# The down projection of a SwiGLU feed-forward layer: eight quarter products, or seven

## The chip, the cores and the metric

One Trainium2 chip; the kernel runs on one of its cores, and all times are device times in microseconds (us). The kernel before has a median of 852.21 us over three runs (851.84 to 852.43). The input is one sequence of 512 tokens with 1024 features, in float32; the weights are float32 and lie in the chip's memory.

## The reference

One decoder layer: three token mixers with gates, a projection with a residual, and a SwiGLU feed-forward layer (FFN) with a residual. The change is in the last line but one, in the product with `ffn_w_down`, a matrix of 2816 x 1024.

```python
def rmsnorm(x, w):
    xf = x.astype(jnp.float32)
    y = xf * lax.rsqrt(jnp.mean(xf * xf, axis=-1, keepdims=True) + EPS)
    return (y * w.astype(jnp.float32)).astype(x.dtype)
...
        x = x + rmsnorm(mixed @ w_out[l], norm_mix_post[l])
        h = rmsnorm(x, norm_ffn_pre[l])
        f = (jax.nn.silu(h @ ffn_w_gate[l]) * (h @ ffn_w_up[l])) @ ffn_w_down[l]
        x = x + rmsnorm(f, norm_ffn_post[l])
```

## The kernel before

All large products are made from float32 numbers that are split into two parts, H (rounded to TensorE's fast float32 form) and L (the rest). A product of two such numbers is three matmuls: H by H, H by L and L by H. A weight chunk of 512 KB goes through `split_chunk`: SyncE issues a DMA into a `raw` buffer, of which there are three (`NRAW`), ScalarE casts it to `wH`, and VectorE subtracts that from `raw` to get `wL`; of `wH` and `wL` there are four buffers each (`NWH`). Since `raw` is read last by the VectorE subtraction, that instruction frees it for the next load.

```python
raw = wpool.tile([P, kt, nf], F32, tag="raw", name=f"raw_{name}", bufs=NRAW)
nc.sync.dma_start(raw, src.rearrange("(k p) f -> p k f", p=P))
S.copy(H, raw)
(eng or V).tensor_tensor(L, raw, H.bitcast(F32), op=ALU.subtract)
```

The FFN begins with 11 steps `u`, each of two blocks of 128 hidden features. A step loads two chunks of the gate weights and two of the up weights (`raw_ffn_w_gate`, `raw_ffn_w_up`, rows of 1 KB in memory), multiplies them with `h2` into the PSUM tiles `ff` (L190), and ends with a SiLU on ScalarE, a product on VectorE (L865) and the split of the result into `gT` (L866, L867).

Then comes the down projection. A chunk is one block of 128 hidden features with all 1024 columns (`raw_fd`, rows of 4 KB). For each of 22 chunks TensorE runs four tiles of 128 tokens x two halves of 512 columns x three parts, 24 matmuls of 128x128 by 128x512 (L201), into eight PSUM banks `dn`; the last three chunks are kept back, so that the four token tiles end one after the other and `post_norm` of a tile (square on ScalarE, power on GpSimd, two products and two sums on VectorE, L219 to L239) runs beside the matmuls of the next. The residual rows come from memory (`x1d`, two loads of 1 MB at L875) and the results go to `out` in halves of 256 KB.

A scheduler places each engine's instructions. It takes the program's order as priorities, and loads and splits of weights stand 400 places ahead of their use (`LEAD`). Each engine then works off its own list in order; SyncE's list holds the DMA issues, and an issue that waits holds up all behind it.

Of the kernel before, what the change touches and what calls it, by code (L numbers as in the profile page):

```python
# [72 lines left out]
def hybrid_block(ctx: ExitStack, tc: tile.TileContext, a: dict, out: bass.AP):
# [595 lines left out]
    def moba(u, qst, kst, vst):  # L669
# [207 lines left out]
    dn = [ps2((NF + t) % 4, f"dn{t}") for t in range(NT)]  # L877
    last = []
    for k in range(NF):
        (h, l, _, _), = load(a["ffn_w_down"][k * P:(k + 1) * P, :], f"fd{k}")  # L880
        W = [(h, l, k, 1)]
        if k >= NF - 3:
            last += W
            continue
# [37 lines left out]
```

## Time and profile before

| what | number |
|---|---|
| median of three runs | 852.21 us (851.84 to 852.43) |
| span of the profiled execution | 850.9 us, 1.3 us under that median |
| instructions | 10857 |
| TensorE busy | 835.4 us, 98% |
| VectorE busy | 411.7 us, 48% |
| ScalarE busy | 302.9 us, 36% |
| GpSimd busy | 64.5 us, 8% |
| bytes moved by DMA | 86.71 MB |

The span is from the first to the last instruction of one profiled execution. Busy times are sums over an engine's instructions without overlaps. The granted clock is the speed that TensorE was given, 1.00 being its full one.

### The profile page before, as it was taken

The page shows a single profiled execution, that of the slowest core. Times are in us where ns is not written, and L with a number is a line of the kernel's source. Part 1 is how long each engine was busy: PE and PEld are TensorE (multiplying, and loading weights), DVE is VectorE, ACT ScalarE, POOL GpSimd, SP SyncE. Part 2 cuts the span into 40 slices and gives each one's busy share as a digit, 9 for nine tenths or more (in the row PEclk, how much of TensorE's full clock was granted, in tenths as well). Part 3 has the DMA queues.
Part 4 walks back from the last instruction along what each step waited for, and adds up shares of the span by engine and source line. Part 5 has one row for each costly group of instructions (what it writes and reads, how often), then busy time and mean ns, then how long its engine had stood idle before and what let it go on. Part 6 is the DMA issues. An engine that isn't in the chain of part 4 may idle for free.

```text
span 850.9 us, 10857 instructions
## 1 busy us (share of the span) xinstructions
PE 835.4 (98%) x4436; PEld 720.8 (85%) x4436; DVE 411.7 (48%) x635; ACT 302.9 (36%) x471; POOL 64.5 (8%) x61
## 2 busy tenths in 40 slices
PE   5999999999999999999999999999999999999997
PEld 5889998889888877888899998888888888888885
DVE  4639957766477564334446553333333333322225
ACT  5354324554455332223344343332222332211112
POOL 2200012110010003112111000000000000000001
PEclk9999999999999999999999999999999999999999
DMA  8421322221322632333351533333333333333302
GB/s 297 124 75 51 84 65 75 75 75 52 100 76 79 217 99 75 99 99 99 99 164 70 172 115 100 99 99 99 100 99 96 94 98 121 113 99 99 99 25 100
DMA packets 70100, 86.71 MB, mean 102 GB/s; under 512 B 3217, under 2 KB 63394, under 8 KB 70050
## 3 DMA queue, kind: packets, MB, share of 16 engines
q1 hardware_dynamic: 70050, 86.01, 33.0%
q8 instruction: 35, 0.57, 0.3%
q14 instruction: 15, 0.12, 0.0%
HBM read 81.81 MB, written 4.19 MB: 101 GB/s over the span
## 4 chain that ended last, share of the span: by engine, by line
PE 96%; DVE 1%; DMA 1%; ACT 0%; POOL 0%; issue 0%; SPq 0%; DVEq 0%; POOLq 0%; ACTq 0%
PE ff L190 28%; PE dn L201 14%; PE ow L201 5%; PE pga L190 5%; PE pgb L190 5%; PE pgc L190 5%; PE gv L201 3%; PE mv L201 3%; PE pya L190 3%; PE mq L190 3%; PE pu L190 3%; PE mk L190 3%; PE pyb L190 3%; PE gqk L190 3%; PE pyc L190 3%; PE gr L201 1%
## 5 line engine op out<-in xcount | busy, mean ns | idle before, releaser
L190 PE MATMUL ff<-h2H,wL_ffn_w_up 128*128 128x512 f32 (+1 forms) x192 | 71.4, 372 | 0.0
L190 PE MATMUL ff<-h2L,wH_ffn_w_up 128*128 128x512 f32 (+1 forms) x192 | 71.3, 372 | 0.0
L190 PE MATMUL ff<-h2L,wH_ffn_w_gate 128*128 128x512 f32 (+1 forms) x192 | 71.2, 371 | 0.0
L190 PE MATMUL ff<-h2H,wL_ffn_w_gate 128*128 128x512 f32 (+1 forms) x192 | 71.2, 371 | 0.0
L190 PE MATMUL ff<-h2H,wH_ffn_w_up 128*128 128x512 f32 (+1 forms) x192 | 71.2, 372 | 0.0
L190 PE MATMUL ff<-h2H,wH_ffn_w_gate 128*128 128x512 f32 (+1 forms) x192 | 71.0, 371 | 0.0
L138 DVE TENSOR_TENSOR wL_fd<-raw_fd,wH_fd 128x1024 fp32r<-128x1024 f32 x22 | 27.0, 1225 | 87.7 <-ACT wH_fd L137 87.7
L138 DVE TENSOR_TENSOR wL_ffn_w_gate<-raw_ffn_w_gate,wH_ffn_w_gate 128x1024 fp32r<-128x1024 f32 x22 | 26.9, 1225 | 75.5 <-ACT wH_ffn_w_gate L137 75.5
L201 PE MATMUL dn<-wH_fd,gTH 128*128 128x512 f32 x160 | 62.2, 389 | 0.0
L201 PE MATMUL dn<-wL_fd,gTH 128*128 128x512 f32 x160 | 62.2, 389 | 0.0
L201 PE MATMUL dn<-wH_fd,gTL 128*128 128x512 f32 x160 | 62.1, 389 | 0.0
L137 ACT CAST wH_fd<-raw_fd 128x1024 fp32r<-128x1024 f32 x22 | 23.2, 1054 | 89.4 <-PE dn L201 74.1
L138 DVE TENSOR_TENSOR wL_ffn_w_up<-raw_ffn_w_up,wH_ffn_w_up 128x1024 fp32r<-128x1024 f32 x22 | 27.0, 1225 | 41.7 <-ACT wH_ffn_w_up L137 41.7
L137 ACT CAST wH_ffn_w_gate<-raw_ffn_w_gate 128x1024 fp32r<-128x1024 f32 x22 | 23.1, 1052 | 56.1 <-issue 34.3
L190 PEld LDWEIGHTS ff<-h2L,wH_ffn_w_up 128*128 128x128 f32 x192 | 36.2, 188 | 6.3
L190 PEld LDWEIGHTS ff<-h2L,wH_ffn_w_gate 128*128 128x128 f32 x192 | 36.2, 188 | 6.3
L190 PEld LDWEIGHTS ff<-h2H,wH_ffn_w_up 128*128 128x128 f32 x192 | 36.1, 188 | 6.3
L190 PEld LDWEIGHTS ff<-h2H,wL_ffn_w_gate 128*128 128x128 f32 x192 | 36.2, 188 | 6.2
L190 PEld LDWEIGHTS ff<-h2H,wL_ffn_w_up 128*128 128x128 f32 x192 | 36.2, 188 | 6.1
L190 PEld LDWEIGHTS ff<-h2H,wH_ffn_w_gate 128*128 128x128 f32 x192 | 36.0, 188 | 6.3
L137 ACT CAST wH_ffn_w_up<-raw_ffn_w_up 128x1024 fp32r<-128x1024 f32 x22 | 23.2, 1053 | 48.8 <-PE ff L190 47.7
L201 PEld LDWEIGHTS dn<-wH_fd,gTH 128*128 128x128 f32 x160 | 30.0, 188 | 6.3
(328 smaller groups left out, 2093.3 us busy)
## 6 DMA issues: line engine op xcount, KB each, us to landing
raw_ffn_w_gate<-in_ffn_w_gate_dram SPq DMA_DIRECT2D x22, 512.0 KB, 3.7
raw_ffn_w_up<-in_ffn_w_up_dram SPq DMA_DIRECT2D x22, 512.0 KB, 3.7
raw_fd<-in_ffn_w_down_dram SPq DMA_DIRECT2D x22, 512.0 KB, 3.4
raw_gatea<-in_w_in_dram SPq DMA_DIRECT2D x8, 512.0 KB, 3.6
raw_gateb<-in_w_in_dram SPq DMA_DIRECT2D x8, 512.0 KB, 3.6
raw_gatec<-in_w_in_dram SPq DMA_DIRECT2D x8, 512.0 KB, 3.5
raw_wo<-in_w_out_dram SPq DMA_DIRECT2D x8, 512.0 KB, 3.5
raw_gv<-in_w_in_dram SPq DMA_DIRECT2D x4, 512.0 KB, 3.5
```

Of the source, the lines that this page charges most:

```text
L137: S.copy(H, raw)
L138: (eng or V).tensor_tensor(L, raw, H.bitcast(F32), op=ALU.subtract)
L190: PE.matmul(ps, lhsT=w[:, k, f * P:(f + 1) * P], rhs=m(k0 + k, lo, hi), start=n == 0 and i == 0, stop=n == len(W) - 1 and i == len(seq) - 1)
L201: PE.matmul(ps, lhsT=m(k0 + k, lo, hi), rhs=w[:, k, c0:c1], start=first and n == 0 and i == 0, stop=last and n == len(W) - 1 and i == len( ...
```

## The change

The down projection is cut into quarters: tokens into two halves of 256, hidden features into two halves of 1408 (11 blocks), columns into two halves of 512. Instead of the eight products of an activation quarter with a weight quarter, seven are made, of sums and differences of quarters: p1, p5, p6, p7, p2, p3, p4 in program order. Each has 11 blocks x two token tiles x three parts, 66 matmuls of the form before, so 462 in place of 528. A chunk of a product is now two blocks by 512 columns (the last one block), again 512 KB, in rows of 2 KB, and is used by 12 matmuls.

Sums of weight quarters are made on VectorE in float32, before the split: t1 of two loads (L946, for p5), t2 = t1 plus a load (L950, for p6), t3 of two loads (L955, for p7), t4 = t2 plus a load (L959, for p4). t1, t2 and t4 stay in a tile `tau`; t3 is made in the raw buffer itself. p1, p2 and p3 use a loaded quarter as it is. The activations stay float32 (`ga`, L893); their sums and differences (L966, L977, L982, L1003) and their splits into H and L (`Quarter.put`: ScalarE L872, VectorE L873) are made in groups of 4, 4 and 3 blocks. p1, p6 and p7 accumulate in the same two PSUM banks, from which ScalarE copies what stands there after each (L972, L987, L991). The residual loads stand at L1020, and `finish` calls `post_norm` for two tiles ahead of p4 and two behind it.

```diff
 NRAW, NWH = 3, 4
 LEAD = 400
 G1W = RANK + 256
+TH = T // 2
+KH = NF // 2
+KGROUPS = ((0, 4), (4, 8), (8, KH))
...
-    def post_norm(pss, wrow, res, dst, name, then):
+    def post_norm(pss, wrow, res, dst, name, then, order=(0, 1)):
+        pss = [pss[c] for c in order]
         rs = rstd_of(pss, [t2(f"sq_{name}_{c}") for c in range(2)], name)
-        sls = [slice(0, T), slice(T, D)]
+        sls = [(slice(0, T), slice(T, D))[c] for c in order]
...
-    gT = Pair(NF, "gT")
+    ga = {(z, i): slot([P, hi - lo, T], f"ga{z}{i}") for z in range(2) for i, (lo, hi) in enumerate(KGROUPS)}
+    def quarter(tz, z, i):
+        return ga[z, i][:, :, tz * TH:(tz + 1) * TH]
+    class Quarter:
...
+        def put(self, i, src):
+            S.copy(self.t[i][:, 0], src)
+            V.tensor_tensor(self.t[i][:, 1], src, self.t[i][:, 0].bitcast(F32), op=ALU.subtract)
...
             S.activation(sg, ff[f][0], AF.Silu)
-            V.tensor_tensor(sg, sg, ff[f][1], op=ALU.mult)
-            S.copy(gT.h(k), sg)
-            V.tensor_tensor(gT.l(k), sg, gT.h(k).bitcast(F32), op=ALU.subtract)
+            V.tensor_tensor(ga[z, r // 4][:, r % 4, :], sg, ff[f][1], op=ALU.mult)
+            if z == 0 and r + 1 in [hi for _, hi in KGROUPS]:
+                a11.put(r // 4, quarter(0, 0, r // 4))
...
+    chunks = [(lo, min(lo + 2, KH)) for lo in range(0, KH, 2)]
...
+    def product(name, X, ps, src, start, group=1):
+        done = []
+        for n, (lo, hi) in enumerate(chunks):
+            with tc.high_priority(offset=LEAD):
+                w = src(n)
+                h = wpool.tile([P, 2, T], F32R, tag="wH", name=f"wH_{name}{n}", bufs=NWH)[:, 0:hi - lo]
+                l = wpool.tile([P, 2, T], F32R, tag="wL", name=f"wL_{name}{n}", bufs=NWH)[:, 0:hi - lo]
+                S.copy(h, w)
+                V.tensor_tensor(l, w, h.bitcast(F32), op=ALU.subtract)
+            done.append((lo, hi, h, l))
+            if n + 1 < len(chunks) and n >= len(chunks) - group:
+                continue
+            for j in range(2):
+                for lo_, hi_, h_, l_ in done:
+                    for k in range(lo_, hi_):
+                        for i, (z, w_) in enumerate(((0, h_), (0, l_), (1, h_))):
+                            PE.matmul(ps[j], lhsT=X.part(z, k, j), rhs=w_[:, k - lo_, :],
+                                      start=start and k == 0 and i == 0, stop=k == KH - 1 and i == 2,
+                                      skip_group_check=True)
+            done = []
+    def raw_of(z, c, name):
+        def src(n):
+            lo, hi = chunks[n]
+            r = wpool.tile([P, 2, T], F32, tag="raw", name=f"raw_{name}{n}", bufs=NRAW)[:, 0:hi - lo]
+            nc.sync.dma_start(r, wq(z, c, lo, hi))
+            return r
+        return src
+    tau = [slot([P, hi - lo, T], f"tau{n}") for n, (lo, hi) in enumerate(chunks)]
+    def t1_of(n):
+        V.tensor_tensor(tau[n], raw_of(0, 0, "t1a")(n), raw_of(0, 1, "t1b")(n), op=ALU.add)
+        return tau[n]
+    def t2_of(n):
+        V.tensor_tensor(tau[n], tau[n], raw_of(1, 1, "t2")(n), op=ALU.add)
+        return tau[n]
+    def t3_of(n):
+        r = raw_of(1, 1, "t3a")(n)
+        V.tensor_tensor(r, r, raw_of(0, 1, "t3b")(n), op=ALU.add)
+        return r
+    def t4_of(n):
+        V.tensor_tensor(tau[n], tau[n], raw_of(1, 0, "t4")(n), op=ALU.add)
+        return tau[n]
+    pa, pc, pd = ps2(0, "pa"), ps2(1, "pc"), ps2(2, "pd")
...
+    for i in NG:
+        V.tensor_tensor(s1[i], quarter(1, 1, i), quarter(1, 0, i), op=ALU.subtract)
+        qs1.put(i, s1[i])
+    product("p1", a11, pa, raw_of(0, 0, "p1"), True)
+    a11.free()
+    cp = [slot([P, 2, T], "c_p")]
+    for j in range(2):
+        S.copy(cp[0][:, j], pa[j])
+    product("p5", qs1, pc, t1_of, True)
...
+    for i in NG:
+        V.scalar_tensor_tensor(s1[i], s1[i], -1.0, quarter(0, 0, i), ALU.mult, ALU.subtract)
+        qs2.put(i, s1[i])
+    product("p6", qs2, pa, t2_of, False)
+    qs3 = Quarter("qs3_")
+    for i in NG:
+        V.tensor_tensor(quarter(0, 0, i), quarter(0, 0, i), quarter(1, 0, i), op=ALU.subtract)
+        qs3.put(i, quarter(0, 0, i))
...
+    for j in range(2):
+        S.copy(cp[1][:, j], pa[j])
+    qs2.free()
+    product("p7", qs3, pa, t3_of, False)
+    for j in range(2):
+        S.copy(cp[2][:, j], pa[j])
+        V.scalar_tensor_tensor(cp[2][:, j], pc[j], -1.0, cp[2][:, j], ALU.mult, ALU.subtract)
...
+    product("p2", a12, pd, raw_of(1, 0, "p2"), True)
...
+    for j in range(2):
+        V.tensor_tensor(cp[0][:, j], pd[j], cp[0][:, j], op=ALU.add)
...
+        V.scalar_tensor_tensor(s1[i], s1[i], -1.0, quarter(0, 1, i), ALU.mult, ALU.subtract)
+        qs4.put(i, s1[i])
...
+    product("p3", qs4, pc, raw_of(1, 1, "p3"), False)
...
-    for t in range(NT):
+    def finish(t, parts, order):
         z = slot([P, D], f"z_{t}")
...
+    for t in range(2):
+        finish(t, [cp[0][:, t], cp[1][:, t]], (0, 1))
+    product("p4", a22, pa, t4_of, False, 2)
+    for t in range(2):
+        finish(2 + t, [pa[t], cp[2][:, t]], (1, 0))
```

The scheduler decides where the new instructions stand. SyncE's list before, at the first loads of the down projection (`raw_fd`, one load a chunk; behind each row, what it waits for: an earlier transfer's landing, or an engine):

```order
L136 DMA raw_fd0_0_5871<-in_ffn_w_down_dram 128x1024 [waits DMAHW0_49,DVE_49]
L136 DMA raw_fd1_0_5901<-in_ffn_w_down_dram 128x1024 [waits DMAHW1_49,DVE_49]
L136 DMA raw_fd2_0_5931<-in_ffn_w_down_dram 128x1024 [waits DMAHW2_49,DVE_49]
L136 DMA raw_fd3_0_5961<-in_ffn_w_down_dram 128x1024 [waits DMAHW3_49,DVE_49]
L136 DMA raw_fd4_0_5991<-in_ffn_w_down_dram 128x1024 [waits DMAHW4_49,DVE_49]
```

And SyncE's list now, from the last load of p1 into those of p5 (`t1a` and `t1b` with a chunk's number, the two quarters of which t1 is the sum):

```order
L939 DMA raw_p15_5928<-in_ffn_w_down_dram 128x512 [waits DMAHW3_49,DVE_49]
L939 DMA raw_t1a0_5942<-in_ffn_w_down_dram 128x2x512 [waits DMAHW4_49,DVE_49]
L939 DMA raw_t1b0_5944<-in_ffn_w_down_dram 128x2x512 [waits DMAHW5_49,DVE_49]
L939 DMA raw_t1a1_5963<-in_ffn_w_down_dram 128x2x512 [waits DMAHW6_49,DVE_49]
L939 DMA raw_t1b1_5965<-in_ffn_w_down_dram 128x2x512 [waits DMAHW7_49,DVE_49]
L939 DMA raw_t1a2_5984<-in_ffn_w_down_dram 128x2x512 [waits DMAHW0_49]
L939 DMA raw_t1b2_5986<-in_ffn_w_down_dram 128x2x512 [waits DMAHW1_49,DVE_49]
```

A chunk of p5 takes two of the three raw buffers; the issue of `t1a2` needs the same VectorE instruction as that of `t1b1` before it, and has no wait for VectorE of its own.

VectorE's list now, from the end of p1's splits (`wL_p15`) to the first split of p5 (`wL_p50`) and a little beyond; `qs2_`, `s1_` and `ga` are activation quarters, `tau` the sums of weights:

```order
L922 TENSOR_TENSOR wL_p15_5931<-raw_p15_5928,wH_p15_5930 128x512 [waits DMAHW6_49,Activation_49]
L982 TENSOR_TENSOR ga01_4275<-ga01_4275 128x4x256 [waits DVE_49]
L873 TENSOR_TENSOR qs2_0_6062<-two_s1_0_5824,qs2_0_6062 128x1024 [waits PE_49,Activation_49]
L982 TENSOR_TENSOR ga02_4276<-ga02_4276 128x3x256 [waits DVE_49]
L946 TENSOR_TENSOR two_tau0_5815<-raw_t1a0_5942,raw_t1b0_5944 128x1024 [waits DMAHW7_49,DMAHW0_49]
L873 TENSOR_TENSOR qs2_1_6063<-two_s1_0_5824,qs2_1_6063 128x1024 [waits Activation_49]
L1003 SCALAR_TENSOR_TENSOR two_s1_0_5824<-two_s1_0_5824,ga10_4277 128x1024 [waits DVE_49]
L922 TENSOR_TENSOR wL_p50_5948<-two_tau0_5815,wH_p50_5947 128x1024 [waits Activation_49]
L1003 SCALAR_TENSOR_TENSOR two_s1_0_5824<-two_s1_0_5824,ga11_4278 128x1024 [waits DVE_49]
L946 TENSOR_TENSOR two_tau0_5815<-raw_t1a1_5963,raw_t1b1_5965 128x1024 [waits DMAHW2_49,DMAHW1_49]
L873 TENSOR_TENSOR qs2_2_6064<-two_s1_2_5825,qs2_2_6064 128x768 [waits PE_49,Activation_49]
L1003 SCALAR_TENSOR_TENSOR two_s1_2_5825<-two_s1_2_5825,ga12_4279 128x768 [waits DVE_49]
```

Before, the same engine had one subtraction a chunk in this stage; now sums and splits of activation quarters that p6 and p3 need stand between p1's last split and p5's first.

SyncE's list now, from the last loads of p7 to those of p2 (`x1_0`, 1 MB, is the residual of the first two token tiles):

```order
L939 DMA raw_t3a5_6302<-in_ffn_w_down_dram 128x512 [waits DMAHW3_49,DVE_49]
L939 DMA raw_t3b5_6304<-in_ffn_w_down_dram 128x512 [waits DMAHW2_49,DVE_49]
L1020 DMA x1_0_6560<-x1d_3725 128x2x1024 [waits DMAHW5_49,PE_49]
L939 DMA raw_p20_6330<-in_ffn_w_down_dram 128x2x512 [waits DVE_49]
L939 DMA raw_p21_6348<-in_ffn_w_down_dram 128x2x512 [waits DMAHW7_49,DMAHW4_49,DVE_49]
```

Before, the residual's first half was loaded during the FFN's first part and its second among the first chunks of the down projection; now the first stands ahead of p2's first chunk, and the second a few loads behind.

## Rows read from the trace of the kernel before

**Rows 1.** The page: each engine's busy us, share of the span and instructions.

```profile
PE 835.4 (98%) x4436; PEld 720.8 (85%) x4436; DVE 411.7 (48%) x635; ACT 302.9 (36%) x471; POOL 64.5 (8%) x61
```

**Rows 2.** The chain of waits at the end: start us, us, what.

```profile
725.09 119.69 PE dn L201 x528
...
844.87 0.60 ACT sq_pf L219
...
845.87 0.59 POOLq L918
...
846.48 0.75 DVE two_z L239
847.23 0.66 DVEq L918
```

**Rows 3.** Table by stretch: down projection, part of the FFN, the end.

```profile
core 0: us, PE busy (x) PEld busy (x) DVE busy (x) ACT busy (x) POOL busy (x), PEclk, DMA share, GB/s
724.93:844.77 119.84, 119.84 (x529) 98.91 (x527) 33.83 (x41) 25.38 (x34) 1.65 (x3) 1.00 0.25 83
495.00:724.00 229.00, 229.00 (x1061) 191.74 (x1060) 81.47 (x87) 71.27 (x89) 0.00 (x0) 1.00 0.35 102
840.00:851.00 11.00, 4.77 (x22) 3.61 (x20) 5.41 (x12) 2.06 (x6) 1.10 (x2) 0.90 0.37 142
```

**Rows 4.** Waits of SyncE's queue: line, for what; total us, times, longest us.

```profile
SPq L136 <- DVE wL_fd L138: 92.5, 19, 5.7
```

**Rows 5.** Landings of raw_fd, then of raw_ffn_w_gate; SyncE's timeline, start and us.

```profile
L136 SPq DMA_DIRECT2D raw_fd<-in_ffn_w_down_dram x22: 327/328/340, 694.6 to 809.1; - x22
...
DMA to landing us min/median/max: 3.1/3.4/5.4
...
L136 SPq DMA_DIRECT2D raw_ffn_w_gate<-in_ffn_w_gate_dram x22: 367/368/384, 439.4 to 678.3; - x22
...
DMA to landing us min/median/max: 3.5/3.7/5.4
...
719.68 0.38 SPq L875 DMA_DIRECT2D x<-x1d  x1
721.80 0.33 SPq L136 DMA_DIRECT2D raw_fd<-in_ffn_w_down_dram  x1
raw_fd<-in_ffn_w_down_dram SPq DMA_DIRECT2D x1, 512.0 KB, 5.4
```

**Rows 6.** Splits and casts in pairs (timeline), then groups by shape with mean ns.

```profile
430.76 1.22 DVE L138 TENSOR_TENSOR wo2L<-raw_wo,wo2H 128x1024 fp32r<-128x1024 f32 x1 [4.63 <-ACT wo2H L137]
431.91 1.22 DVE L138 TENSOR_TENSOR wL_wo<-raw_wo,wH_wo 128x1024 fp32r<-128x1024 f32 x1
...
429.68 1.05 ACT L137 CAST wo2H<-raw_wo 128x1024 fp32r<-128x1024 f32 x1 [2.32 <-DMA raw_wo<-in_w_out_dram]
430.64 1.05 ACT L137 CAST wH_wo<-raw_wo 128x1024 fp32r<-128x1024 f32 x1
...
L138 DVE TENSOR_TENSOR wL_fd<-raw_fd,wH_fd 128x1024 fp32r<-128x1024 f32 x22 | 27.0, 1225 | 87.7 <-ACT wH_fd L137 87.7
L865 DVE TENSOR_TENSOR sg<-sg,ff 128x512 f32<-128x512 f32 x22 | 15.1, 687 | 13.0 <-PE ff L190 12.9
L867 DVE TENSOR_TENSOR gTL<-sg,gTH 128x512 fp32r<-128x512 f32 x20 | 13.7, 688 | 6.2 <-ACT gTH L866 6.2
```

**Rows 7.** DMA issues with us to landing; the DMA's rate from 8 to 20 us.

```profile
out_dram<-two_z SPq DMA_DIRECT2D x6, 256.0 KB, 2.0
...
DMA packets 3895, 4.55 MB, mean 379 GB/s; under 512 B 700, under 2 KB 3407, under 8 KB 3895
```

**Rows 8.** VectorE's timeline at the end: start us, us.

```profile
845.67 0.69 DVE L237 TENSOR_TENSOR two_z<-dn,two_wp 128x512 f32<-128x512 f32 x1
846.48 1.41 DVE L239 SCALAR_TENSOR_TENSOR two_z<-two_z,rs_pf,x 128x512 f32<-128x512 f32 x2
```

More of the change, by code (lines that the diff above doesn't have):

```diff
@@ L851, in hybrid_block, with __init__, part, free @@
     free("xr_0", "xr_2", "wn", "wo2H", "wo2L", "wo3H", "wo3L")
-    gT = Pair(NF, "gT")
+    ga = {(z, i): slot([P, hi - lo, T], f"ga{z}{i}") for z in range(2) for i, (lo, hi) in enumerate(KGROUPS)}
+    def quarter(tz, z, i):
+        return ga[z, i][:, :, tz * TH:(tz + 1) * TH]
+    class Quarter:
+        def __init__(self, name):
+            self.t = [slot([P, 2, hi - lo, TH], f"{name}{i}", F32R) for i, (lo, hi) in enumerate(KGROUPS)]
+            self.names = [f"{name}{i}" for i in range(len(KGROUPS))]
+        def put(self, i, src):
+            S.copy(self.t[i][:, 0], src)
+            V.tensor_tensor(self.t[i][:, 1], src, self.t[i][:, 0].bitcast(F32), op=ALU.subtract)
+        def part(self, z, k, j):
+            return self.t[k // 4][:, z, k % 4, j * P:(j + 1) * P]
+        def free(self):
+            free(*self.names)
+    a11 = Quarter("a11")
     for u in range(NF // 2):
@@ L869, in hybrid_block, with wq @@
     h2.free()
+    wd = a["ffn_w_down"]
+    chunks = [(lo, min(lo + 2, KH)) for lo in range(0, KH, 2)]
+    NG = range(len(KGROUPS))
+    def wq(z, c, lo, hi):
+        r = (z * KH + lo) * P
+        return wd[r:r + (hi - lo) * P, c * T:(c + 1) * T].rearrange("(k p) f -> p k f", p=P)
+    def product(name, X, ps, src, start, group=1):
[18 more added lines that the diff above has]
+            done = []
@@ new lines, in t3_of @@
+    def t3_of(n):
[6 more added lines that the diff above has]
+    pa, pc, pd = ps2(0, "pa"), ps2(1, "pc"), ps2(2, "pd")
+    s1 = [slot([P, hi - lo, TH], f"s1_{i}") for i, (lo, hi) in enumerate(KGROUPS)]
+    qs1 = Quarter("qs1_")
+    for i in NG:
+        V.tensor_tensor(s1[i], quarter(1, 1, i), quarter(1, 0, i), op=ALU.subtract)
+        qs1.put(i, s1[i])
@@ new lines, in hybrid_block @@
+    product("p1", a11, pa, raw_of(0, 0, "p1"), True)
[4 more added lines that the diff above has]
+    product("p5", qs1, pc, t1_of, True)
+    qs1.free()
+    qs2 = Quarter("qs2_")
+    for i in NG:
[6 more added lines that the diff above has]
+        qs3.put(i, quarter(0, 0, i))
@@ new lines, in hybrid_block @@
+    free(*[f"ga0{i}" for i in NG])
+    cp += [slot([P, 2, T], "c_u2"), slot([P, 2, T], "c_u3")]
+    for j in range(2):
[5 more added lines that the diff above has]
+        V.scalar_tensor_tensor(cp[2][:, j], pc[j], -1.0, cp[2][:, j], ALU.mult, ALU.subtract)
+    a12 = Quarter("a12")
+    for i in NG:
+        a12.put(i, quarter(0, 1, i))
+    product("p2", a12, pd, raw_of(1, 0, "p2"), True)
@@ new lines, in hybrid_block @@
+    a12.free()
+    qs3.free()
+    for j in range(2):
+        V.tensor_tensor(cp[0][:, j], pd[j], cp[0][:, j], op=ALU.add)
+    qs4 = Quarter("qs4_")
+    for i in NG:
+        V.scalar_tensor_tensor(s1[i], s1[i], -1.0, quarter(0, 1, i), ALU.mult, ALU.subtract)
+        qs4.put(i, s1[i])
+    free(*[f"s1_{i}" for i in NG])
+    product("p3", qs4, pc, raw_of(1, 1, "p3"), False)
+    for j in range(2):
+        V.scalar_tensor_tensor(cp[1][:, j], pc[j], -1.0, cp[1][:, j], ALU.mult, ALU.subtract)
@@ L870, in hybrid_block @@
+    qs4.free()
+    a22 = Quarter("a22")
+    for i in NG:
+        a22.put(i, quarter(1, 1, i))
+    free(*[f"ga1{i}" for i in NG])
     wp = slot([P, D], "wp")
@@ L876, in hybrid_block @@
         x1 += [xt[:, 0], xt[:, 1]]
[L877 to L884, printed above, removed]
-        for t in range(NT):
-            for c in range(2):
-                mm_tm(dn[t][c], gT, t, W, c * T, (c + 1) * T, k == 0, False)
-    for t in range(NT):
-        for c in range(2):
-            mm_tm(dn[t][c], gT, t, last, c * T, (c + 1) * T, False, True)
-    for t in range(NT):
-        z = slot([P, D], f"z_{t}")
-        post_norm(dn[t], wp, x1[t], z, f"pf{t}",
-                  lambda sl: nc.sync.dma_start(out[t * P:(t + 1) * P, sl], z[:, sl]))
+    def finish(t, parts, order):
+        z = slot([P, D], f"z_{t}")
+        post_norm(parts, wp, x1[t], z, f"pf{t}",
+                  lambda sl: nc.sync.dma_start(out[t * P:(t + 1) * P, sl], z[:, sl]), order)
+    for t in range(2):
[3 more added lines that the diff above has]
+        finish(2 + t, [pa[t], cp[2][:, t]], (1, 0))
 _INS = ["x", "norm_mix_pre", "w_in", "gla_w_g2", "gla_b_g", "gla_norm", "pool_w", "pool_scale",
```

1 line of the change is left out of this document (added).

## The prediction, made from the kernel before

> **What bounds the kernel now.** I read the page first: TensorE is busy for 98% of the span and VectorE for 48% [rows 1]. Next the chain of waits: the down projection is one unbroken piece of 528 matmuls in 119.69 us, so one matmul of 512 columns costs 119.69 / 528 = 0.2267 us of the path, although each is recorded with 389 ns, because they overlap; after its last matmul the chain runs through a square, a power and two sums of one tile [rows 2]. The table by stretch says the same of the engines there: TensorE 119.84 of 119.84 us, VectorE 33.83, ScalarE 25.38, all at a granted clock of 1.00, and DMA at a share of 0.25 [rows 3]. So this stage is bound by TensorE alone, and work beside it is free while it keeps up.
>
> Then what feeds TensorE. SyncE, which issues the loads, waited 19 times for the VectorE split that frees a raw buffer, the longest 5.7 us: it is paced by the 24 matmuls (5.44 us) of a chunk [rows 4]. A load lands 3.1, 3.4 or 5.4 us (shortest, median, longest) after its issue with rows of 4 KB, and 3.5, 3.7, 5.4 with rows of 1 KB [rows 5]. One split of 128x1024 on VectorE takes 1.225 us; two in a row start 1.15 us apart (430.76, 431.91), and the ScalarE casts 0.96 us apart [rows 6].
>
> **What it removes.** 528 matmuls become 7 x 66 = 462 of the same 512 columns. 66 x 0.2267 = 15.0 us. Two ScalarE casts and VectorE splits per FFN tile pair also change, but those engines have room there (VectorE 81.47 of 229 us, [rows 3]), which I cost at nothing: the cover is TensorE at 229.00 of 229.00.
>
> **What it adds, product by product.** The program order of TensorE is p1, p5, p6, p7, p2, p3, p4, each 66 x 0.2267 = 14.96 us if fed. A chunk is now 12 matmuls, 2.72 us, in place of 24, and p5 and p7 need two loads and one VectorE add for each chunk. Only three raw buffers exist. Two hold the pair being added and the third the first half of the next pair; the second half (t1b, t3b) can be issued only when the add has freed a buffer. So add, load, add, load is one serial loop: 1.225 (the add, by the split's row of like size) + 0.03 + 3.5 (landing, with rows of 2 KB between 3.4 and 3.7) = 4.75 us a chunk against TensorE's 2.72. The last chunk is half as big: 0.69 (the 128x512 row, [rows 6]) + 0.03 + 2.7 (estimate: between 2.0 for the stores of 256 KB, [rows 7], and 3.5) = 3.4 us.
>
> - *p1*: its first chunks are split before the FFN ends; no loss.
> - *p5*: the last product of the FFN (L893) waits for the FFN's last matmul, so it stands at p1's start; one difference is ahead of it and 15 instructions behind it up to the first split of p5 (the third fence of the change shows the end of that row of work). Of the 17, eleven have 1024 elements at 1.15, four 768 at 0.88 (estimate between 0.61 and 1.15), two 512 at 0.61 (0.688 less the 0.07 by which two overlap): 17.4 us, and TensorE needs 14.96 for p1. The split is 2.3 us late. The second add has two quarter operations ahead of it: 1.1 us more. Then four loops of 4.75, one of 3.4, and 0.9 for the last four matmuls: 2.3 + 1.1 + 19.0 + 3.4 + 0.9 = 26.7 us in place of 14.96, **+11.7**.
> - *p6*: one load per chunk, but VectorE has to add (5 x 1.15 + 0.61 = 6.4), split (6.4), split five pieces of later quarters that stand between (3 x 1.15 + 2 x 0.88 = 5.2) and finish p5's last split (0.6): 18.6 us against 14.96, **+3.7**.
> - *p7*: the same loop as p5. Its first add stands about 5 us ahead of p6's end, since VectorE is a chunk and a half (4.1 us) ahead of TensorE plus one split. From that add: four loops and the short one (22.4), then add, cast and split of the half chunk (2.0) and 0.9 of matmuls, less 5.0: 20.3 us, **+5.3**.
> - *p2*: SyncE's queue now has a 1 MB load of x1 between the last t3 loads and p2's first one (the fourth fence of the change). That chunk is issued after p7's fifth split, lands after 3.5 + 0.7 (a share of the 2.8 us that 1 MB takes at 379 GB/s, [rows 7]), is cast 1.05 and split 1.225: 6.5 us, while TensorE has 3.7 us of p7 left and 0.4 of matmuls that need the cast only: **+2.4**.
> - *p3, p4*: one load a chunk at 1.15 + 1.15 us of VectorE work and few quarters; 2.72 us of TensorE covers them: no loss. Each of p2, p3 and p4 then needs 2.88 MB in 15 us, half of 379 GB/s.
> - *Tail*: before, one tile is finished after the last matmul (844.77 to 850.9, 6.1 us, [rows 3]). Now two tiles end within two matmuls of each other, and the second one's product and two sums (0.69 + 1.41, [rows 8]) stand behind the first's on VectorE: between 0 and 2.3 us, taken as **+1.9**, nearer the upper end because both wait for the last two matmuls.
>
> Sum: -15.0 + 11.7 + 3.7 + 5.3 + 2.4 + 1.9 = +10.0 us. On the profiled span of 850.9 that is 860.9. The median of the runs shown is 852.21, 1.3 us over that span; with the same 1.3 the forecast is **862.2 us**, 1.2% slower.
>
> **Bounds.** The loop runs eight times in full and twice at half size, counted as nine. With the shortest landing, 3.1, it costs 9 x 0.4 = 3.6 us less; with the longest, 5.4, 17 us more. The raw_fd that took 5.4 us was issued at 721.80, two us after a 1 MB load (719.68, [rows 5]), so loads that meet others are late, and here they come in pairs; half of that, +8, is my upper end. VectorE's 1024-element operations on the quarters read rows of 256 in place of 1024; no row has this form, and I keep the price of the split, since where the operand lies did not matter in two other forms (128x512 from PSUM 687 ns, from SBUF 688, [rows 6]). Its other uncertain pieces (p6, the 1.1) move 3 us either way.
>
> **Rivals.**
> 1. *Not slower: the loads run ahead and the loop never closes.* If SyncE gets far enough ahead during p1, and the loop costs less than TensorE's chunk, only p6, p2, the first split and the tail remain: -15.0 + 3.7 + 2.4 + 2.3 + 1.9 = -4.7, 847.5 us; without the first three too, 839. The point from which it decides: -15.0 + 10.3 leaves 4.7 us for ten loops, so a loop under 2.72 + 0.5 = 3.2 us, a landing under 2.0. The trace has no 512 KB load under 3.1 [rows 5]. For it: the queue was idle for three quarters of this stage before [rows 3]. Chance 0.07.
> 2. *The pairs land late.* Every second load comes right behind another, as that 5.4 us one did; the loop is then 5.7 to 6.6 us. At +1.0 for nine loops and p2: 872 us. For it: 5.4 also is the longest of the FFN's loads. Against: the second of a pair has a whole loop of time. Chance 0.14.
> 3. *TensorE's clock falls.* In p5 and p7 it would be idle for 2 of each 4.75 us. The granted clock is 1.00 over the whole stage before, its level of 2.4 GHz, and 0.90 over the last 11 us, in which TensorE is busy for 4.77 and then has stopped for good [rows 3]; no row shows it with work in short bursts. The Trainium skill (TensorE: Matmul & The Clock Gate, "HAM oscillation — how this bites in real kernels") describes a kernel whose loop over chunks waited for a load each time, and whose clock fell at every chunk; no run here shows that so far. At 1.2 GHz twelve matmuls would cost 5.4 us, over the loop's 4.75, so p5 and p7 would take 30 us each (+3.3, +9.6): 875 us. Against: the idle pieces are about 2 us, with 2.7 us of work between them. Chance 0.05.
>
> The forecast itself has 0.74. That VectorE alone would bind is no case of its own: over the seven products it has some 110 us of work (44 of splits, 25 of adds, 19 of quarter splits, 13 of quarter sums, 10 of the rest, at the prices above) against TensorE's 105, and a part of it runs before p1. Where it binds most, in p6, it is in the sum.
>
> **How the numbers follow.** The forecast reaches from 856 (short landings, p6 cheaper) to 869; adding rival 2 up to 872 and a little of the low side gives 855 to 872, which leaves out most of rivals 1 and 3 and the upper half of 2: some 0.18. A measurement here tells 0.2%, 1.7 us, from no change. Faster: 0.06; same: 0.02; slower: 0.92.
>
> **What would show it.** In the changed kernel's profile the window of p5 and p7 should have TensorE idle between chunks with VectorE's split as releaser, SyncE waiting for the adds (L946, L955), issues of t1b 4.5 to 5 us apart, VectorE busy for nearly all of p6, p3 and p4 with TensorE full, and 462 down matmuls. A p5 of under 18 us breaks the loop; landings over 4.5 us speak for rival 2, a granted clock under 1.00 between p5 and p7 for rival 3. It is wrong altogether if TensorE stays full through p5.

## The result, and the profile after

The changed kernel takes 873.62 us (median of four runs, 872.37 to 875.19) against 852.04 us for the kernel before on the same chip (median of four now): a ratio of 1.0253, 95% interval 1.0239 to 1.0266. It is slower, as forecast, but by twice as much: the profiled span went from 850.9 to 870.6 us, +19.7, where the sum had +10.0, and 873.62 lies above the range of 855 to 872.

The table by stretch of the changed kernel, one row for each product (p1, p5, p6, p7, p2, p3, p4, in TensorE's order) and one for the tail; it answers to [rows 3]. A row is 66 matmuls in TensorE's order; at the end of p5 two of p6's stand ahead of p5's last four, so that border is sharp to half a microsecond only:

```profile
core 0: us, PE busy (x) PEld busy (x) DVE busy (x) ACT busy (x) POOL busy (x), PEclk, DMA share, GB/s
724.28:739.24 14.96, 14.96 (x68) 12.33 (x66) 14.96 (x16) 7.73 (x9) 0.00 (x0) 1.00 0.35 107
739.24:766.01 26.77, 17.98 (x67) 11.53 (x67) 19.66 (x19) 10.35 (x12) 0.00 (x0) 1.00 0.60 209
766.01:785.97 19.96, 15.77 (x67) 12.04 (x65) 19.52 (x19) 9.86 (x12) 0.00 (x0) 1.00 0.55 179
785.97:813.11 27.14, 18.67 (x67) 12.55 (x67) 13.80 (x15) 8.94 (x11) 0.00 (x0) 0.94 0.73 233
813.11:830.46 17.35, 16.82 (x67) 13.47 (x67) 10.28 (x10) 7.76 (x9) 0.00 (x0) 0.90 0.76 263
830.46:845.42 14.96, 14.96 (x68) 12.39 (x66) 12.51 (x16) 7.06 (x10) 0.00 (x0) 1.00 0.62 205
845.42:862.75 17.33, 15.79 (x67) 12.04 (x65) 15.55 (x22) 7.40 (x14) 2.72 (x2) 1.00 0.32 117
862.75:870.60 7.85, 0.00 (x1) 0.00 (x0) 4.32 (x9) 1.52 (x6) 1.10 (x2) 0.66 0.37 142
```

A product that TensorE sets takes 14.96 us; p1 and p3 do. So each row's first number less 14.96 is what that product lost. Beside the forecast's terms (us):

| part | forecast | measured |
|---|---|---|
| 66 matmuls fewer | -15.0 | -15.0 |
| p1 starts (724.28, before 725.09) | 0 | -0.8 |
| p5 | +11.7 | +11.8 |
| p6 | +3.7 | +5.0 |
| p7 up to its last matmul | +5.3 | +7.7 |
| wait for p2's first chunk, and p2 | +2.4 | +6.8 |
| p3 | 0 | 0 |
| p4 | 0 | +2.4 |
| tail | +1.9 | +1.7 |
| sum | +10.0 | +19.6 |

p7's row is 27.14 us because it holds the wait for p2's first chunk: p7's last matmul starts at 808.44, and with one matmul's 0.23 us it ends at 808.67. p7 without the wait, the wait, and a stretch soon after it:

```profile
785.97:808.67 22.70, 18.50 (x66) 12.54 (x66) 12.49 (x12) 7.08 (x9) 0.00 (x0) 0.92 0.68 211
808.67:813.11 4.44, 0.16 (x2) 0.00 (x1) 1.31 (x3) 1.86 (x3) 0.00 (x0) 1.00 0.96 348
815.00:817.30 2.30, 2.30 (x7) 1.82 (x6) 1.85 (x2) 0.64 (x1) 0.00 (x0) 0.50 0.86 270
```

In the wait TensorE is idle while the DMA engines are busy for 96%; in the last row TensorE works at a granted clock of 0.50, its level of 1.2 GHz.

The chain of waits shows the loop in p5 (start us, us, what):

```profile
742.37 1.23 DVE two_tau L946
...
743.62 3.72 DMA raw_t1b<-in_ffn_w_down_dram
...
747.43 1.24 DVE two_tau L946
...
748.69 3.55 DMA raw_t1b<-in_ffn_w_down_dram
```

And through p7, with what came behind it:

```profile
785.27 1.24 DVE raw_t3a L955
...
786.52 4.02 DMA raw_t3b<-in_ffn_w_down_dram
...
790.63 1.24 DVE raw_t3a L955
...
791.88 3.85 DMA raw_t3b<-in_ffn_w_down_dram
...
804.87 7.06 DMA raw_p<-in_ffn_w_down_dram
...
812.01 1.05 ACT wH_p L921
```

Add, load, add, load, with nothing else between: the forecast's loop. Its adds start at 785.27, 790.63, 795.75 and 801.23, 5.1 to 5.5 us apart. Then one load of p2 takes 7.06 us. The landings (us from issue) of the second loads of p5, of those of p7, and of the loads issued from 803 to 810:

```profile
DMA to landing us min/median/max: 2.8/3.3/3.7
...
DMA to landing us min/median/max: 3.8/3.9/4.1
...
x<-x1d SPq DMA_DIRECT2D x2, 1024.0 KB, 6.9
raw_p<-in_ffn_w_down_dram SPq DMA_DIRECT2D x3, 512.0 KB, 7.1
```

### The profile page after: what moved, and what is told of

The parts are those of the page before. It is cut to its first block, busy times and chain, and to the rows that moved or that the text cites. A ratio compares the mean times of both kernels' runs of the same rounds, so it can differ in the third digit from the quotient of the medians.

```text
span 870.6 us, 10892 instructions
## 1 busy us (share of the span) xinstructions
PE 829.3 (95%) x4370; PEld 706.8 (81%) x4370; DVE 481.3 (55%) x696; ACT 329.5 (38%) x496; POOL 66.0 (8%) x61
## 4 chain that ended last, share of the span: by engine, by line
PE 81%; DVE 8%; DMA 7%; issue 2%; ACT 1%; POOL 0%; SPq 0%; DVEq 0%; POOLq 0%; ACTq 0%
PE ff L193 27%; PE ow L204 5%; PE pga L193 5%; PE pgb L193 5%; PE pgc L193 5%; PE gv L204 3%; PE mv L204 3%; PE pya L193 3%; PE mq L193 3%; PE pu L193 3%; PE mk L193 3%; PE pyb L193 3%; PE gqk L193 3%; PE pyc L193 2%; DVE wL_p L922 2%; DMA raw_p<-in_ffn_w_down_dram 2%
## 5 line engine op out<-in xcount | busy, mean ns | idle before, releaser
L930 PE MATMUL pa<-wH_p,qs 128*128 128x512 f32 x88 | 29.6, 409 | 3.8 <-ACT wH_p L921 3.6
L922 DVE TENSOR_TENSOR wL_p<-raw_p,wH_p 128x1024 fp32r<-128x1024 f32 (+1 forms) x18 | 20.3, 1134 | 21.6 <-ACT wH_p L921 21.4
L229 POOL TENSOR_TENSOR rs_pf<-ms_pf,half 128x1 f32<-128x1 f32 x4 | 3.8, 961 | 372.7 <-DVE ssq_pf L226 366.8
L930 PE MATMUL pc<-wH_p,qs 128*128 128x512 f32 x88 | 28.6, 395 | 3.3 <-ACT wH_p L921 3.3
L921 ACT CAST wH_p<-two_tau 128x1024 fp32r<-128x1024 f32 (+1 forms) x18 | 17.5, 975 | 29.3 <-DVE two_tau L946 16.6
L921 ACT CAST wH_p<-raw_p 128x1024 fp32r<-128x1024 f32 (+1 forms) x18 | 17.5, 978 | 27.7 <-DMA raw_p<-in_ffn_w_down_dram 13.7
```

The source lines that it names most:

```text
L229: pows.append(G.tensor_tensor(rs, ms, half[:, 0:1], op=ALU.pow))
L921: S.copy(h, w)
L922: V.tensor_tensor(l, w, h.bitcast(F32), op=ALU.subtract)
L930: PE.matmul(ps[j], lhsT=X.part(z, k, j), rhs=w_[:, k - lo_, :], start=start and k == 0 and i == 0, stop=k == KH - 1 and i == 2, skip_group ...
```

## The experiments

The theory was that the add-load-add loop paces p5 and p7, and VectorE's queue p6. Its rivals were that VectorE alone paces all three, that the loads as such come too late, and that the clock takes the time. Where a span is compared, it is that of one profiled execution; the changed kernel's, 870.6, belongs to the shortest of its four runs.

### One loop opened: the first load straight into tau

```diff
-        V.tensor_tensor(tau[n], raw_of(0, 0, "t1a")(n), raw_of(0, 1, "t1b")(n), op=ALU.add)
+        nc.sync.dma_start(tau[n], wq(0, 0, *chunks[n]))
+        V.tensor_tensor(tau[n], tau[n], raw_of(0, 1, "t1b")(n), op=ALU.add)
```

> The first load of every pair of p5 (t1a) goes straight into the tile tau, and the add runs in place; only t1b uses the three raw buffers. No instruction of VectorE is taken away. Theory (the add-load-add loop on the raw buffers paces p5): p5 falls from 26.8 us to what VectorE needs there, 19.7, or up to 21; p7 keeps its loop (adds 5.1 to 5.5 us apart); total -6 to -8 us. Rival (VectorE's own work paces p5): p5 stays over 24 us. Rival (the pairs land late because two loads share the memory): loads of t1b take over 4.5 us and p5 stays over 24 us.

863.14 us (862.29 to 864.68), ratio 1.0133 (1.0118 to 1.0149), so about -10.5 against the changed kernel, more than the 6 to 8 expected. p5, p6 and p7 of this run:

```profile
739.91:762.18 22.27, 18.34 (x67) 14.27 (x66) 22.27 (x22) 11.58 (x13) 0.00 (x0) 0.85 0.52 166
762.18:777.52 15.34, 15.12 (x67) 12.20 (x65) 15.34 (x16) 8.82 (x11) 0.00 (x0) 1.00 0.45 137
777.52:803.41 25.89, 19.14 (x66) 12.44 (x66) 14.28 (x15) 8.95 (x11) 0.00 (x0) 0.93 0.71 239
```

p5 fell by 4.5 us, a little less than expected, and p6 by 4.6, which I had not expected; a likely reason is that VectorE came out of p5 further ahead. p7, whose loop was left as it was, still lost 10.9 with the wait behind it (12.2 in the changed kernel). Same bytes, same VectorE instructions, another buffer: the loop paced p5. What remains of p5 is VectorE's, busy 22.27 of 22.27 us. Behind a wait of 3.80 us for the second split the clock fell, and twelve matmuls came 0.2 us later each.

### The second loads left out

```diff
-        V.tensor_tensor(tau[n], raw_of(0, 0, "t1a")(n), raw_of(0, 1, "t1b")(n), op=ALU.add)
+        r = raw_of(0, 0, "t1a")(n)
+        V.tensor_tensor(tau[n], r, r, op=ALU.add)
...
-        V.tensor_tensor(r, r, raw_of(0, 1, "t3b")(n), op=ALU.add)
+        V.tensor_tensor(r, r, r, op=ALU.add)
```

> Leaves out the second load of every pair: t1 and t3 are the first quarter added to itself, so VectorE has as many instructions of the same size as before. Theory (loop): p5 at 19 to 21 us as in the run that loads into tau, p7 from 22.7 to 15 to 17 us, and p2 starts less late; total -12 to -18 us. Rival (VectorE's work): p5 stays over 24 and p7 over 21 us. With fewer idle pieces in p7 the granted clock should stay at 1.00 there, if these bring it down.

The sums are then other ones; only the time is read. 854.14 us (853.89 to 856.56), about -19.5, a little more than the 12 to 18 expected. p5 took 21.06 us, as expected, p6 15.8, p7 20.22 in place of 15 to 17, at a granted clock of 0.92: a miss for my expectation of the clock. p7 has two waits (0.82 and 1.82 us by the rows), and behind the second its matmuls came 0.43 us apart in place of 0.23.

### Both loops undone, the result kept

```diff
-        r = raw_of(1, 1, "t3a")(n)
-        V.tensor_tensor(r, r, raw_of(0, 1, "t3b")(n), op=ALU.add)
+        r = raw_of(0, 0, "t3a")(n)
+        V.tensor_tensor(r, tau[n], r, op=ALU.subtract)
```

This stands on the edit of the first experiment: t3 is t2 less the first quarter, so one load does.

> Undoes both loops with the result kept: t1a goes straight into tau, and t3 is made as t2 minus the first quarter, one load a chunk in place of two. VectorE has the same number of instructions. Theory (loops): close to the run that left out the second loads, whose span was 852.9 us: p5 21, p6 15 to 16, p7 18 to 20, p4 17 to 18 us, span 851 to 855. What is left over then is VectorE's (p5's second split stands behind seven instructions). Rival (the second loads themselves, by their bytes, not the loop): p5 over 23 us, since t1a and t1b are both still loaded.

853.59 us (852.03 to 854.09), ratio 1.0012 (1.0003 to 1.0022), span 852.3: the loops, with what came of them, cost 18 (span) to 20 us (medians), and without them the change about breaks even. In p7 this takes the loop away together with its second load; no run opens p7's loop with all its bytes, so there the loop rests on the chain of waits above and on p5's experiment. p1, p5, p6 and p7:

```profile
724.90:739.86 14.96, 14.96 (x67) 12.39 (x66) 14.96 (x16) 7.56 (x8) 0.00 (x0) 1.00 0.43 140
739.86:760.93 21.07, 17.14 (x68) 13.37 (x66) 21.07 (x21) 11.60 (x13) 0.00 (x0) 0.92 0.52 162
760.93:776.72 15.79, 15.43 (x67) 12.12 (x66) 15.79 (x16) 10.12 (x12) 0.00 (x0) 1.00 0.37 117
776.72:794.46 17.74, 15.95 (x66) 12.41 (x67) 14.15 (x14) 6.73 (x8) 0.00 (x0) 1.00 0.50 148
```

From p1's first matmul to p6's end VectorE is busy for 14.96 + 21.07 + 15.79 = 51.82 of 51.82 us, and TensorE needs 3 x 14.96 = 44.9. The 6.9 between them are what p5 and p6 lost. On TensorE's side it is mostly one wait, for p5's second split, which stands behind seven other instructions of VectorE (3.8 us), and what half clock behind that wait cost (1.7 us). So behind the loops stands VectorE, the rival that the prediction had set aside. That VectorE is full doesn't show this alone, since it also works ahead for p7; the last two experiments test it.

### The quarters' splits on GpSimd

```diff
-        def put(self, i, src):
+        def put(self, i, src, eng=None):
             S.copy(self.t[i][:, 0], src)
-            V.tensor_tensor(self.t[i][:, 1], src, self.t[i][:, 0].bitcast(F32), op=ALU.subtract)
+            (eng or G).tensor_tensor(self.t[i][:, 1], src, self.t[i][:, 0].bitcast(F32), op=ALU.subtract)
```

> The subtraction in Quarter.put runs on GpSimd, the loads stay. Theory (loop in p5 and p7, VectorE in p6): p5 loses only its late head, to 23 to 24 us, p6 falls from 20.0 to 15 to 16 us, the adds of p7 stay 5.1 to 5.5 us apart and p7 at 21 to 23 us; total -6 to -9 us. Rival (VectorE's work paces all three): p5 and p7 fall to 15 to 18 us. Rival (GpSimd and VectorE disturb each other): VectorE's splits take over 1.3 us and nothing is won.

885.31 us (884.64 to 887.1), ratio 1.0395: slower by 11.7 than the changed kernel. The third expectation, that the two engines disturb each other, was the right one. VectorE's timeline in p6, then GpSimd's:

```profile
769.29 2.17 DVE L950 TENSOR_TENSOR two_tau<-two_tau,raw_t 128x1024 f32<-128x1024 f32 x1 [1.17 <-DMA raw_t<-in_ffn_w_down_dram]
772.12 3.27 DVE L950 TENSOR_TENSOR two_tau<-two_tau,raw_t 128x1024 f32<-128x1024 f32 x1
775.32 2.83 DVE L922 TENSOR_TENSOR wL_p<-two_tau,wH_p 128x1024 fp32r<-128x1024 f32 x1
778.07 1.21 DVE L950 TENSOR_TENSOR two_tau<-two_tau,raw_t 128x1024 f32<-128x1024 f32 x1
```

```profile
767.48 2.89 POOL L873 TENSOR_TENSOR qs<-ga,qs 128x1024 fp32r<-128x1024 f32 x1 [8.42 <-ACT qs L872]
771.53 2.78 POOL L873 TENSOR_TENSOR a<-ga,a 128x1024 fp32r<-128x1024 f32 x1 [1.16 <-DVE two_tau L950]
774.27 2.79 POOL L873 TENSOR_TENSOR qs<-ga,qs 128x768 fp32r<-128x768 f32 x1
```

The add that starts at 772.12 takes 3.27 us: GpSimd's subtraction ends at 774.31, and 1.1 us later the add is done (775.39). The split of 775.32 ends at 778.15, 1.1 us after GpSimd's next (777.06). The add of 769.29 ends at 771.46, again 1.1 us after GpSimd's (770.37). With GpSimd idle, at 778.07, the same add takes 1.21. So in these rows VectorE's instruction makes next to no way until GpSimd's is done. Work moved to GpSimd was not taken off VectorE's time: from p1 to p2 VectorE was busy for 85.1 us, against 78.2 in the changed kernel. How the 11.7 us divide between this, GpSimd's slower subtractions (2.4 to 2.9 us each) and a lower clock (0.83 in p5) is not separated.

### The residual's loads

Left out:

```diff
-    x1 = []
-    for t in range(0, NT, 2):
-        xt = slot([P, 2, D], f"x1_{t}")
-        nc.sync.dma_start(xt, x1d[t * P:(t + 2) * P, :].rearrange("(t p) f -> p t f", p=P))
-        x1 += [xt[:, 0], xt[:, 1]]
...
-        post_norm(parts, wp, x1[t], z, f"pf{t}",
+        post_norm(parts, wp, wp, z, f"pf{t}",
```

> Leaves out the two loads of the residual (the sum at the end adds the norm's weights in its place). Theory (the 1 MB loads delay p2's first chunk): that load lands in 4 to 5 us and not 7.06, the 4.4 us in which TensorE waits between p7 and p2 fall to about 2, the granted clock in p2 stays at 1.00, p2 at 15 to 16 us; total -4 us. Rival (p2's own three loads, issued one after the other, are enough): the load still takes over 6.5 us and the gap stays over 4 us.

872.06 us (871.5 to 872.33), 1.6 less in the median where 4 was expected. p2's first load took 4.98 us in place of 7.06 and the wait ahead of p2 was 2.35 us in place of 4.44: that half was right. But p2 still had a clock of 0.90 and took 17.50 us, and p7 lost 0.7 us more and p4 0.9, so the profiled span is the same (870.5).

Moved ahead instead (the same five lines, put ahead of the copies of `cp[1]`):

> The loads of the residual stand further ahead in the program: one between the loads of p6, one ahead of those of p7, none ahead of p2. Theory (they delayed p2's first load): it lands in 4.5 to 5.5 us and not 7.06, the gap between p7 and p2 is about 2 us and not 4.4; p6 or p7 takes up to 1 us more, since the loads now meet theirs; total -1 to -3 us. Rival (the place does not matter, the 2 MB cost the same anywhere in this stage): p6 and p7 longer by what p2 wins.

869.97 us (868.42 to 871.25), about -3.6 in the median and -1.1 in the profiled span. p2's first load took 4.88 us, the wait 2.2 us, and p2 16.42 us at a clock of 1.00. p6, which now met the first of these loads, took 22.88 us in place of 19.96, with a clock of 0.85, where at most 1 more was expected. Its load that met them, and the split that waited for it:

```profile
764.24 8.84 DMA raw_t<-in_ffn_w_down_dram
...
774.33 1.15 DVE wL_p L922
```

TensorE went on behind that split 1.2 us later than in the changed kernel, counted from the first split. The other 1.6 us are a fall of the clock behind this wait, and that is not shown to be the loads' doing: in the next experiment p6 falls too, with the loads in their old place. So a part of the cost went where the loads went, as the rival had it.

### TensorE kept busy in p7

```diff
+            for _ in range(fill[n + 1 == len(chunks)]):
+                PE.matmul(pf[0], lhsT=X.part(0, 0, 0), rhs=done[-1][2][:, 0, :], start=True, stop=True)
...
-    product("p7", qs3, pa, t3_of, False)
+    product("p7", qs3, pa, t3_of, False, fill=(5, 14))
```

> Adds matmuls whose result nobody reads (a PSUM bank not in use otherwise): 5 behind each of the first five chunks of p7 and 14 behind its last, where TensorE was idle for about 2.5 us and 4.4 us in the changed kernel. Theory (the idle pieces of p7 bring the granted clock down, and that costs time where TensorE is full again, in p2): the clock stays at 1.00 through p7 and p2, p2 falls from 17.35 to 15.8 to 16.2 us, p7's adds stay 5.1 to 5.5 us apart; total -1 to -2 us. Rival (the clock falls for another reason): half-rate matmuls in p2 as before, no change. Rival (the added matmuls are in the way): p7 longer by over 1 us.

871.66 us (870.7 to 873.45). p6, p7 and p2 of this run:

```profile
766.29:788.57 22.28, 18.32 (x72) 14.36 (x71) 19.94 (x19) 10.61 (x13) 0.00 (x0) 0.92 0.51 162
788.57:814.08 25.51, 23.34 (x101) 18.54 (x100) 12.35 (x12) 7.51 (x9) 0.00 (x0) 1.00 0.72 246
814.08:829.04 14.96, 14.96 (x67) 12.39 (x66) 10.74 (x11) 8.39 (x11) 0.00 (x0) 1.00 0.87 293
```

With matmuls in the idle pieces the clock stays at 1.00 through p7 and p2, and p2 takes exactly 14.96 us; p7 and p2 together 40.47 in place of 44.49. Of these 4.0 us p2 has 2.4, and p7 with the wait behind it 1.6; there p7's first add also stood further ahead (7.7 us before p7's start, 5.3 in the changed kernel). Another thing moved with it: the second residual load was issued behind p2's first chunks (814.48 in place of 808.90), and p2's first load landed in 4.9 us. That alone doesn't raise p2's clock, since without the residual's loads p2 had the same short landing and 0.90. So TensorE kept busy kept its clock here; the mean clock was 0.996 in three of the four runs and 0.991 in one, against 0.991 to 0.995 in the changed kernel. What idle piece brings it down is not shown: p6, where nothing was added, this time fell to 0.92 and took 2.3 us more, with the same two waits (1.57 and 2.39 us) at which the changed kernel's p6 kept 1.00 (1.60 and 2.38), and p2 of the run before this one kept 1.00 behind a wait of 2.2 us with nothing added. What tips it is open.

### Two versions without what was found

On top of both loops undone: the difference of L982 is made in place during the FFN, right behind `a11.put`, and the residual's loads stand early.

```diff
                 a11.put(r // 4, quarter(0, 0, r // 4))
+                V.tensor_tensor(quarter(0, 0, r // 4), quarter(0, 0, r // 4), quarter(1, 0, r // 4), op=ALU.subtract)
...
-    V.scalar_tensor_tensor(s1[i], s1[i], -1.0, quarter(0, 0, i), ALU.mult, ALU.subtract)
+    V.scalar_tensor_tensor(s1[i], quarter(1, 1, i), -1.0, quarter(0, 0, i), ALU.mult, ALU.subtract)
```

> As the run with both loops undone, and besides the three differences of the first token half's quarters are made in place during the FFN, when VectorE has room, and the residual's loads stand ahead of p7's. Theory (after the loops, VectorE's queue between p1 and p6 is what binds): 3.2 us of VectorE work leave this stretch, p5 falls to 17 to 19 us, p6 and p7 to 15 to 17, p2 to 15; span 842 to 847 us, median 843 to 849, faster than the kernel before. Rival (VectorE's queue does not bind there): p5 stays at 21 us and the span over 850.

847.63 us (846.93 to 848.12), ratio 0.9943 (0.9931 to 0.9956): faster than the kernel before. p5 took 17.55 us, p6 16.57, p7 15.13, p2 15.68, and the clock was 1.00 in all of them. Two things changed at once, but p5 ends before the residual's loads are issued (760.43), so its 3.5 us come from the moved differences: in place of the wait of 3.8 us it has two, of 0.7 and 1.3, and no fall of the clock behind them. p4 took 18.51.

Then the norm's weights ahead of the FFN, in a free buffer:

```diff
     a11 = Quarter("a11")
+    wp = [t2(f"wp{c}", tag="mix") for c in range(2)]
+    for c in range(2):
+        nc.sync.dma_start(wp[c], rows(a["norm_ffn_post"][c * T:(c + 1) * T], T))
...
```

> As the run with the differences in the FFN and the residual early, and besides the norm's weights are loaded ahead of the FFN into a free buffer, so that the first products of the two early tiles can run in p3. Theory (p4's 3.5 us over come from VectorE: four of these products, 2.4 us, stood between the first add and the first split of p4, behind a load that landed at its start): p4 falls from 18.5 to 16 to 17 us, all else as before, median 845 to 847 us. Rival (p4 waits for its own loads): p4 stays at 18 us or more, and the median within 1 us of 847.6.

846.2 us (845.13 to 846.56), ratio 0.9924 (0.991 to 0.9937), the best of all. p5, p6 and p4:

```profile
739.75:757.30 17.55, 15.55 (x67) 12.23 (x66) 17.55 (x18) 9.68 (x12) 0.00 (x0) 1.00 0.55 175
757.30:773.85 16.55, 15.75 (x68) 12.05 (x66) 16.55 (x17) 9.11 (x11) 0.00 (x0) 1.00 0.73 260
819.26:836.88 17.62, 15.93 (x67) 11.97 (x65) 16.17 (x23) 7.52 (x14) 3.05 (x2) 1.00 0.39 128
```

p4 fell by 0.9, less than the 1.5 to 2.5 expected. VectorE's timeline at p4's start shows why:

```profile
814.96 1.22 DVE L965 TENSOR_TENSOR two_tau<-two_tau,raw_t 128x1024 f32<-128x1024 f32 x1
818.61 1.23 DVE L965 TENSOR_TENSOR two_tau<-two_tau,raw_t 128x1024 f32<-128x1024 f32 x1 [2.44 <-DMA raw_t<-in_ffn_w_down_dram]
819.75 1.22 DVE L927 TENSOR_TENSOR wL_p<-two_tau,wH_p 128x1024 fp32r<-128x1024 f32 x1
```

The first split of p4 (819.75) stands behind the second add, which waits 2.44 us for its load, although its own add was done at 816.2. So both sides of that test hold a part: the products were in the way, and so is a load. VectorE is full in p5 and p6 still (17.55 and 16.55 us).

## Why the prediction was right and wrong

**Right: the direction, and the loop.** Three raw buffers, two of them held by an add, make a serial loop; p5 came out at 26.77 us against 26.7 forecast, its landings in the chain at 3.72, 3.55 and 3.31 us against 3.5, and opening the loop in p5 alone took it out there and left it in p7. The marks named for it were there: TensorE idle between chunks, SyncE waiting for the add (six times for L946, 23.0 us in all), and issues of t1b at 743.62, 748.69, 753.58 and 758.17, 4.6 to 5.1 us apart. TensorE's waits in p5 ended with a cast nearly as often as with a split. The tail (+1.7 against +1.9) and p3 were right too. That p5's sum fits to 0.1 us is luck in part: 17.4 less 14.96 is 2.4 and not 2.3; from the first split to the fifth it took 19.2 us where I had 20.1, and the last, short step took 4.9 where I had 3.4, because p6's first add, which waited for its load, and a quarter's split stood ahead of it.

The sum missed 9.6 us. Of these, p2 and the wait ahead of it have 4.4, p7 2.4, p4 2.4 and p6 1.3; p1 and the tail gave 1.0 back.

**Wrong: the price of p2's first chunk, +6.8 in place of +2.4.** The mechanism was right, the 1 MB load in front, but its term was mis-sized. I took the chunk's landing as 3.5 us and a quarter of a 1 MB transfer, 4.2 us. It took 7.06: two more chunks of p2 and the second 1 MB load followed within 4 us, and the transfers shared the engines (348 GB/s over the wait, near the 379 of [rows 7]). Without the residual's loads it took 4.98, so they had 2.1 of it; the sum had 0.7 for them, and nothing for p2's own next chunks. The landing is 2.9 of the 4.4 us. About 1.5 are the clock, which the sum left at 1.00: 0.50 from 815.0 to 817.3, and p2 at 14.96 us when TensorE was kept busy ahead of it.

**Wrong: one loop price for both.** I used 4.75 us for p5 and p7 alike. In p5 the second load is issued first, when the add frees its buffer, and lands in 3.3 us (median). In p7 the sum is made in the raw buffer, so the split, not the add, frees it; the next pair's first load is then issued 1.3 to 3.1 us ahead of the second, and the second lands in 3.9 us (median). That this order makes it later is argued; no run changes the order alone. From the first add (780.64) to the last (805.34) it took 24.7 us where I had 22.4; that is what p7 lost more. Four full steps took 20.6 us where I had 19.0. The last took 4.1 where I had 3.4, because it begins with the add of a full chunk (1.24 us), and my sum put the half chunk's add there (0.69). Rival 2 (pairs that land late) had the direction here, but not its 5.4 us.

**Wrong: p4 at nothing, and p6 too low.** p4 was costed by one add and one split a chunk. In the trace its splits stand behind adds for later chunks, the first behind one that waited 1.28 us for its load, and the third behind two sums with p3's result as well (L1008). TensorE waited 0.44 us for the one and 1.10 for the other; the rest of the 2.4 us is not read apart:

```profile
844.06 1.22 DVE L959 TENSOR_TENSOR two_tau<-two_tau,raw_t 128x1024 f32<-128x1024 f32 x1 [1.28 <-DMA raw_t<-in_ffn_w_down_dram]
...
849.75 1.28 DVE L1008 SCALAR_TENSOR_TENSOR two_c_u<-pc,two_c_u 128x512 f32<-128x512 f32 x2
853.35 0.50 PE L930 MATMUL pa<-wL_p,a 128*128 128x512 f32 x1 [1.10 <-DVE wL_p L922]
```

p6 was costed as a sum of VectorE's work, 18.6 us; VectorE was busy for 19.52 of its 19.96. But the order made the waits: TensorE waited 1.60 us for the first split and 2.38 for the second, the last row but one here, and from there it worked to p6's end without a wait.

```profile
768.08 1.22 DVE L873 TENSOR_TENSOR a<-ga,a 128x1024 fp32r<-128x1024 f32 x1
769.22 1.22 DVE L950 TENSOR_TENSOR two_tau<-two_tau,raw_t 128x1024 f32<-128x1024 f32 x1
770.35 0.95 DVE L873 TENSOR_TENSOR qs<-ga,qs 128x768 fp32r<-128x768 f32 x1
771.22 1.22 DVE L950 TENSOR_TENSOR two_tau<-two_tau,raw_t 128x1024 f32<-128x1024 f32 x1
772.36 1.22 DVE L922 TENSOR_TENSOR wL_p<-two_tau,wH_p 128x1024 fp32r<-128x1024 f32 x1
773.63 0.50 PE L930 MATMUL pa<-wL_p,qs 128*128 128x512 f32 x1 [2.38 <-DVE wL_p L922]
```

The other price in this count held: VectorE's operations on quarters in rows of 256 take 1.22 us, like the split; those of 768 elements 0.95 us, starting 0.87 apart (estimate 0.88).

**Rival 3, the clock,** had been given 0.05 with p5 and p7 at 30 us. It fell, but in pieces of a few microseconds; in p7 it was 0.92 by the mark that I had named for this rival, but there the loop left room and it cost nothing; in p2 it cost about 1.5 us. The longer runs of the changed kernel have the lower clock: spans of 870.6 us at a mean of 0.993 and 0.995, of 873.0 and 873.4 at 0.991. The Trainium skill (TensorE: Matmul & The Clock Gate, "HAM oscillation — how this bites in real kernels") describes a kernel that waited some 3 to 5 us for loads at each chunk and whose clock fell at every one. The loop here has shorter waits, and the traces don't show a fall at every chunk: p5 of the changed kernel, with no wait over 1.52 us, ran its 26.77 us at 1.00.

**VectorE as a bound,** which the prediction did not count as a case of its own, is what is left when the loops are gone (full from p1 to p6's end, 6.9 us over TensorE; taking 3.2 us of its work out of there took 3.5 off p5). The forecast counted part of it, as p5's late head and p6.

## What to carry to other kernels

Fewer products with sums in front move the work to the engine that makes the operands, so count that engine for each product against the matmuls saved, and look at the order of its queue, not only at its sum. When an operation needs two buffers of a ring of three, the second load waits for the operation: load one operand straight into the place where the sum stays, or derive the sum from one that is there. Where TensorE has waited, ask for the clock in the stretch behind it, since that is where its price shows.

## What the runs showed of the hardware

While GpSimd made a subtraction, VectorE's two-input instructions that started behind it were held until it was done: 1.22 us became 2.2 to 3.3 us. The Trainium skill (SBUF — State Buffer, "Who interferes with whom") says that a VectorE instruction with two inputs in SBUF contends with a GpSimd instruction that reads SBUF, that this contention is an exclusive lock, and that the order of issue decides who blocks. The rows of that experiment agree: GpSimd's instruction had started first each time, and VectorE's ended 1.08 to 1.09 us behind its end (774.31 to 775.39, 777.06 to 778.15). Here the move of the splits made the kernel 11.7 us slower.
